# First-layer activations of token tiles five to nine and the scaling of rows on ScalarE instead of VectorE, with a planner that reckons with later landings

## The chip, the cores and the metric

The kernel runs on one core of a Trainium2 chip. A core has five instruction streams: PE (TensorE, matrix products; its weight loads are shown as PEld), DVE (VectorE), ACT (ScalarE), POOL (GpSimd) and SP (SyncE, which here issues nearly all transfers). The metric is the device time of one execution in microseconds (us); lower is better. Runs of this kernel differ by about 0.2%, which is about what a measurement can tell from no change.

## What is computed

Two layers of a diffusion backbone over 1024 latent tokens and 256 context tokens, width 1024, in float32. Cut to what matters here:

```python
for i in range(2):
    mod_x = silu(c) @ w_mod[i] + b_mod[i]          # shift, scale, gate for the latent tokens
    mod_c = silu(c_ctx) @ w_mod[i] + b_mod[i]      # and for the context tokens
    hx = rms_norm(x, norm_g[i]) * (1 + sc_x) + sh_x
    hc = rms_norm(ctx, norm_g[i]) * (1 + sc_c) + sh_c
    if i == 0:   # grouped-query attention, 16 heads on 4 key/value heads, per-head norm of q and k, 2-D rotary
        yx, yc = gqa_axial_mixer(hx, hc, a_w_in, a_q_norm_g, a_k_norm_g, a_w_out, cos, sin, True)
    else:        # neighbourhood attention (8 x 16 window plus all context tokens) with a position bias
        yx, yc = neighbourhood_mixer(hx, hc, b_w_in, b_rpb, b_w_out, False)
    # each mixer: (attention * silu(z)) @ w_out
    x = x + g_x * yx
    ctx = ctx + g_c * yc     # first layer only
return rms_norm(x, final_norm_g)
```

## The kernel before

Tokens lie in ten tiles of 128: tiles 0 to 7 are the latent tokens, 8 and 9 the context. A float32 operand of a product is split into two float16 parts, hi and lo, and a product is three matmuls (hi*hi, hi*lo, lo*hi).

**The first stage** (to about 100 us) loads `w_m0` (the modulation weights), the tokens and the key/value weights, and makes the first layer's input and its keys and values. `ln_pre(t)` loads a token tile, takes the sum of squares on ACT (L867), the inverse root on POOL (L660), and scales the rows in place by that factor on DVE (L869). `mod_cols` gives, for each block `kt` of 128 channels, the scale and shift columns `acol` and `scol`. `h_kt(t0, n, kt)` then makes one block of the input for `n` token tiles: PE transposes into a PSUM bank `pl` (L876), ACT writes hi as scale times value plus shift (L881), DVE writes the same in float32 into `tf` (L882), and DVE subtracts hi to get lo (L883):

```python
S.activation(hi[:, kt, c], pv, AF.Identity, scale=a, bias=b)      # L881
V.tensor_scalar(tf, pv, a, b, op0=ALU.mult, op1=ALU.add)          # L882
V.tensor_tensor(lo[:, kt, c], tf, hi[:, kt, c], op=ALU.subtract)  # L883
```

The calls are `h_kt(t, 1, 0)` for t = 0 to 3, `h_kt(0, 4, kt)` for kt = 1 to 7, `h_kt(4, 1, kt)`, `h_kt(5, 3, kt)` (384 columns) and `h_kt(8, 2, kt)` (256 columns) for all eight kt. The bank `pl` is one of two with the tag "pj". `kv_mm` multiplies the input with the key/value weights (PE L887, accumulators `pkv`), `kv_post` normalises and rotates k (mostly DVE), and `load_w` splits weights (ACT L730, DVE L731; `wkv`, then `wa` for the queries).

**The first layer** (about 100 to 700 us) projects queries and gates (PE L1034, `pa`), forms scores (`pm` for row maxima, `st`), and attends. `q_att` does one head of each pair with queries on the partitions: scores (`qs`, L1186 and L1187), DVE copies them with a running maximum into `qpf` (L1190), ACT takes the exponentials into the float16 tile `qpp` and back into `qpf` (L1202, L1203), POOL subtracts for the lo part (L1130), SP transposes by DMA within the tile `qpp` (L1205), and PE multiplies with the values (`qpv`, L1211 and L1213). `qpp` has four buffers, `qpf` four.

**The turn of the layers** (about 700 to 810 us) does the output projection (`poa`, L1358), the second normalisation (`ln_rows`, `split_rows`: DVE L677, L678, L690), and the first products of the second layer in a Winograd-like scheme (`winograd`: banks `pwq0a`, `pwq0b`, `pwq0c`; ACT copies `e1q` from the first at L1457; DVE makes `w1q` and `w2q` from `e1q` and the second at L1461 and L1469, after which PE goes on in that bank, L1517).

**The second layer** (about 810 to 1300 us) projects (`pwq`, `pwv`) and attends (`b_att`): scores `bsn` and `bsc`, exponentials into `bph` on ACT, the lo part on POOL (L1130), a DMA transpose `bpht<-bph` on SP (L1641), and the product with the values (`bpv`, L1646 to L1649). `bph` has four buffers, `bpht` six. The last stage is the output projection `pob` (L1739) with the final norm.

**What sets the order.** `Planner` walks over all instructions, keeps a modelled clock for each engine, and lays each engine's instructions in the order in which its model starts them; `apply` then pins this order on every queue. `cost` gives each instruction's modelled occupancy and latency; `schedule` adds semaphore delays, buffers, and for transfers a landing time: a DMA is taken to be usable 1500 ns after its share of the DMA engines is through. `deadlines` works out by when each instruction is needed so that PE does not wait, with a margin, and `refine` plans five more times with these due times as the rank, keeping the shortest plan. So an edit to the planner moves instructions on all five queues of the whole program.

Of the kernel before, what the change touches and what calls it, by code (L numbers as in the profile page):

```python
# [15 lines left out]
AF = mybir.ActivationFunctionType  # L16
ALU = mybir.AluOpType
# [25 lines left out]
class Planner:  # L43
# [2 lines left out]

    ENG = {"PE": "PE", "DVE": "DVE", "Activation": "ACT", "Pool": "POOL", "SP": "SP"}
    AHEAD = 2000.0
    SEM = {"PE": 60.0, "DVE": 35.0, "ACT": 35.0, "POOL": 80.0, "SP": 30.0}

    def __init__(self, tc, first=0):
# [64 lines left out]
    def cost(self, x, rd, wr):  # L116
# [6 lines left out]
        if e == "PE":  # L123
            f32 = ins[0].dtype == mybir.dt.float32
            cols = self.elems(outs[0])
            passes = (2 if x.is_transpose else 4) if f32 else 1
            if f32 and any("idf" in a.bass_ap.tensor.name for a in ins):
                passes = 2
            return max(cols * passes / 2.4 + 2.5, 29.0), 170.0
        if k == "InstDmaTransposeAnt":  # L130
            m = 1
            for s, c in list(ins[0].ap):
# [155 lines left out]
        self.gone = set(gone)  # L288

    def schedule(self, key=None, margin=0.0, scale=None):  # L290
        scale = scale or {}
        N = len(self.node)
        rank = key or (lambda i: i)
        key = lambda i: -1 if i in self.glued else rank(i)
# [20 lines left out]
        t = dict.fromkeys(engs, 0.0)  # L315
# [40 lines left out]
        while count < N:  # L356
# [43 lines left out]
            if e == "PE":  # L400
                ts, tp = tuple(x.tile_size or (128, 128)), tuple(x.tile_position or (0, 0))
                if pe_last and pe_last[0] != ts:
                    s += 97
                fin = s + occ + lat
                if ts[1] < 128 and pe_last and pe_last[0] == ts and pe_last[1] != tp:
                    t[e] = max(s + 7, t[e])
                    pe_hold = max(pe_last[2], s + occ)
                    t[e] = s + 7
                    pe_last = (ts, tp, pe_hold)
                else:  # L410
                    if pe_last and pe_last[0] == ts and ts[1] < 128:
                        pass
                    t[e] = s + (occ if ts[1] == 128 else occ / 4)
                    pe_last = (ts, tp, s + occ)
            elif type(x).__name__ in ("InstDMACopy", "InstDmaTransposeAnt"):
                t[e] = s + occ
                dma = max(dma, s + occ) + lat
                fin = dma + 1500
            else:
                t[e] = s + occ  # L420
                fin = s + occ + lat
# [34 lines left out]
    def deadlines(self, margin):  # L456
# [4 lines left out]
        for a in self.order["PE"]:  # L461
            idle += max(0.0, start[a] - prev)
            prev = max(prev, start[a] + (cst[a][0] if tuple(self.node[a].tile_size or (128, 128))[1] == 128
                                         else cst[a][0] / 4))
            due[a] = start[a] - idle
        heirs = collections.defaultdict(list)
        for i, names in self.came.items():
# [56 lines left out]
def trunk_kernel(ctx, tc, x, cx, cc, norm_g, ng_row, b_cols, sel_c, w_m0, w_mb, b_mod, a_wkv, a_wq, a_qg, a_kg, a_w_out,  # L524
# [337 lines left out]
    def ln_pre(t):  # L862
        xt = xstage[t] if t < NX else lp.tile([P, D], F32, name=f"xt{t}", tag="xt", bufs=2)
        DM.dma_start(xt, x[t * P:(t + 1) * P, :] if t < NX else cx[(t - NX) * P:(t - NX + 1) * P, :])
        jk = lp.tile([P, D], BF16, name=f"xj{t}", tag="xj", bufs=1)
        ss = lp.tile([P, 1], F32, name=f"xss{t}", tag="lss", bufs=2)
        S.activation(jk, xt, AF.Square, accum_out=ss)  # L867
        rs = rstd_from(lp, ss, 1, 1.0 / D, EPS, "ln")
        V.tensor_scalar_mul(xt, xt, rs[:, 0:1])  # L869
        xts[t] = xt  # L870

    def h_kt(t0, n, kt):
# [6 lines left out]
        pv = ps.rearrange("p a b -> p (a b)")  # L879
        a, b = acol[0][:, kt, s:s + 1], scol[0][:, kt, s:s + 1]  # L880
        S.activation(hi[:, kt, c], pv, AF.Identity, scale=a, bias=b)  # L881
        V.tensor_scalar(tf, pv, a, b, op0=ALU.mult, op1=ALU.add)  # L882
        V.tensor_tensor(lo[:, kt, c], tf, hi[:, kt, c], op=ALU.subtract)  # L883

    def kv_mm(ps, t, kt):
# [959 lines left out]
```

## Time and profile before

| what | us |
|---|---|
| median of 3 runs | 1345.55 (1344.1 to 1347.17) |
| the profiled execution | 1345.52 |
| its span, first to last instruction | 1343.7 |
| mean granted TensorE clock | 0.992 of full speed |

The profiled execution's own time lies 1.8 us above its span; the span is what the views divide up. "PE busy" counts the modelled duration of pipelined matmuls, so a short wait between two of them may not show as idle. In the busy tenths PE is at 8 or 9 in every one of 40 slices but the last (6); DVE stands at 79% of the span, ACT at 72%, POOL at 66%.

### The profile page before, as it was taken

What the parts mean: (1) busy time and instruction counts of PE and PEld (TensorE: products, weight loads), DVE (VectorE), ACT (ScalarE), POOL (GpSimd) and SP (SyncE); (2) the same over time, 40 slices, a digit from 0 to 9 for tenths busy, and PEclk for the clock granted to TensorE, in tenths of its full rate; (3) what the DMA queues carried; (4) which work ended last, traced back from release to release, by engine and by line L of the source; (5) the groups of instructions that cost most, each with busy time, mean ns of one, the idle gap of its engine ahead of it and who ended that gap; (6) DMA issues with size and microseconds to landing.
All of it is one profiled execution on the core that took longest, in us unless ns stands there. A gap on an engine that the chain in (4) does not pass through costs nothing.

```text
span 1343.7 us, 38645 instructions
## 1 busy us (share of the span) xinstructions
PE 1309.6 (97%) x15100; PEld 928.6 (69%) x15100; DVE 1067.1 (79%) x2456; ACT 969.0 (72%) x2076; POOL 891.2 (66%) x1214
## 2 busy tenths in 40 slices
PE   8999999999999999999999989999999999999996
PEld 4457777777777777776654457869687786968552
DVE  5898787888889787769528997878888888887665
ACT  4554889988888777798743456878878888887453
POOL 2323878777777767687876467677676868767543
PEclk9899999999999999999999999999999999999998
DMA  9633576786675222244317962678777877669952
GB/s 371 188 116 96 111 152 117 145 187 135 140 145 122 74 67 72 59 119 108 113 51 187 243 139 82 125 145 152 150 139 142 158 143 162 145 151 226 286 130 110
DMA packets 390496, 191.64 MB, mean 143 GB/s; under 512 B 349792, under 2 KB 355104, under 8 KB 390312
## 3 DMA queue, kind: packets, MB, share of 16 engines
q1 hardware_dynamic: 389736, 189.13, 62.1%
q8 instruction: 118, 1.93, 0.6%
q14 instruction: 66, 0.54, 0.1%
q10 hardware_dynamic: 576, 0.03, 0.0%
HBM read 91.03 MB, written 15.75 MB: 79 GB/s over the span
## 4 chain that ended last, share of the span: by engine, by line
PE 73%; DVE 10%; ACT 6%; DMA 5%; issue 3%; POOL 2%; DVEq 0%; POOLq 0%; SPq 0%; ACTq 0%
PE pa L1034 13%; PE poa L1358 6%; PE pob L1739 6%; PE st L1260 3%; PE st L1261 3%; PE pm L1068 3%; PE pkv L887 2%; PE pv L1137 2%; PE pv L1138 2%; PE pv L1136 2%; DMA bpht<-bph 2%; DMA qpp<-qpp 2%; PE pvc L1577 1%; PE qpv L1211 1%; PE pbc L1527 1%
## 5 line engine op out<-in xcount | busy, mean ns | idle before, releaser
L1130 POOL TENSOR_TENSOR pl<-pf,ph 128x256 f16<-128x256 f32 x400 | 274.9, 711 | 85.7 <-ACT pf L1247 56.2
L1130 POOL TENSOR_TENSOR bph<-bpf,bph 128x256 f16<-128x256 f32 (+1 forms) x224 | 184.0, 848 | 102.0 <-ACT bpf L1637 81.8
L1034 PE MATMUL pa<-wa,x 128*128 128x256 f16 x1536 | 219.8, 272 | 0.7 <-DVE q L822 0.7
L1245 ACT ACTIVATE ph<-st 128x512 f16<-128x512 f32 x240 | 143.8, 602 | 58.0 <-PE st L1261 56.2
L1565 PEld LDWEIGHTS <-hx 128*128 128x128 f16 x2688 | 157.3, 98 | 10.2 <-issue 1.3
L1034 PEld LDWEIGHTS <-x 128*128 128x128 f16 x1536 | 140.4, 97 | 33.3 <-issue 1.4
L1247 ACT ACTIVATE pf<-st 128x512 f32<-128x512 f32 x240 | 143.6, 604 | 2.0 <-DVE pl L1127 0.9
L1069 DVE TENSOR_REDUCE mxp<-pm 128x1 f32<-128x512 f32 x192 | 127.3, 683 | 12.8 <-PE pm L1068 11.7
L1137 PE MATMUL pv<-v,ph 128*128 128x64 f16 x960 | 122.4, 195 | 0.0
L1136 PE MATMUL pv<-v,ph 128*128 128x65 f16 x960 | 121.9, 193 | 0.2 <-ACT ph L1245 0.2
L1138 PE MATMUL pv<-v,pl 128*128 128x65 f16 x960 | 121.3, 192 | 0.0
L1130 POOL TENSOR_TENSOR qpp<-qpf,qpp 128x256 f16<-128x256 f32 (+1 forms) x158 | 93.4, 616 | 31.6 <-ACT qpf L1203 29.3
L1517 PEld LDWEIGHTS <-wb 128*128 128x128 f16 x672 | 63.9, 98 | 71.9 <-issue 6.6
L1635 ACT ACTIVATE bph<-bpf,bnx 128x384 f16<-128x384 f32 (+1 forms) x128 | 69.3, 581 | 52.4 <-DVE bnx L1627 33.8
L1136 PEld LDWEIGHTS <-ph 128*128 128x128 f16 x960 | 90.9, 97 | 22.1 <-ACT ph L1245 0.7
L1137 PEld LDWEIGHTS <-ph 128*128 128x128 f16 x960 | 90.4, 97 | 15.8 <-issue 0.4
L1138 PEld LDWEIGHTS <-pl 128*128 128x128 f16 x960 | 91.2, 99 | 9.3 <-POOL pl L1130 1.2
L1260 PE MATMUL st<-q,k 128*128 128x512 f16 x240 | 90.8, 379 | 0.7 <-ACT pf L1247 0.4
L1261 PE MATMUL st<-q,k 65*128 65x512 f16 x240 | 91.5, 381 | 0.0
L1358 PE MATMUL poa<-woa,oa 128*128 128x512 f16 x384 | 89.8, 379 | 0.0
L1739 PE MATMUL pob<-wob,obf 128*128 128x512 f16 x336 | 80.5, 379 | 1.9 <-DVE acc L1742 1.4
L1434 POOL TENSOR_TENSOR wtb<-wsb 128x256 f32<-128x256 f32 x64 | 56.5, 884 | 32.5 <-DMA wsb<-in_b_wp 17.0
(485 smaller groups left out, 4050.2 us busy)
## 6 DMA issues: line engine op xcount, KB each, us to landing
wg<-in_w_mb SPq DMA_DIRECT2D x32, 512.0 KB, 4.5
wsb<-in_b_wp SPq DMA_DIRECT2D x64, 256.0 KB, 2.8
wm<-in_w_m SPq DMA_DIRECT2D x16, 512.0 KB, 9.0
wsa<-in_a_wq SPq DMA_DIRECT2D x32, 256.0 KB, 3.5
xstage<-in_x SPq DMA_DIRECT2D x8, 512.0 KB, 5.6
wsoa<-in_a_w_out SPq DMA_DIRECT2D x16, 256.0 KB, 2.7
x<-in_x SPq DMA_DIRECT2D x8, 512.0 KB, 8.5
x_d<-x SPq DMA_DIRECT2D x8, 512.0 KB, 5.1
```

Of the source, the lines that this page charges most:

```text
L1034: T.matmul(ps[:, :, i, :], hA(a, kt, t), wt[w][:, kt, :], start=n == 0, stop=n == 3 * KT - 1)
L1130: G.tensor_tensor(lo[:, c], p32[:, c], hi[:, c], op=ALU.subtract)
L1136: T.matmul(pv[:, t, :], hi[:, c], v[:, 0:65], start=first and t == 0, stop=False)
L1137: T.matmul(pv[:, t, 0:HD], hi[:, c], v[:, 65:129], start=False, stop=False)
L1138: T.matmul(pv[:, t, :], lo[:, c], v[:, 0:65], start=False, stop=last and t == n - 1)
L1245: S.activation(ph, st, AF.Exp)
L1247: S.activation(p32, st, AF.Exp)
L1260: T.matmul(so, k1[:, g, kc], q1[:, :, i, :], start=True, stop=False)
L1261: T.matmul(so, k2[0:65, g, kc], q2[0:65, :, i, :], start=False, stop=True)
L1358: T.matmul(ps, lhs(a, kt), w[b][:, kt, :], start=n == 0, stop=n == 3 * KT - 1)
L1565: T.matmul(ps[:, t * P:(t + 1) * P], hx[a][:, t, blk, kt], wt[j][:, s_, w, kt], start=first and t == 0 and m == 0, stop=last and t == 3 an ...
L1739: T.matmul(ps, ob[kt][:, t, a], wout["b"][hf][b][:, kt, :], start=n == 0, stop=n == 3 * len(kts) - 1)
```

## The change

Three things, of which the third moves everything:

1. In `ln_pre` the scaling of the rows stays on DVE for tiles 0 to 3 and goes to ACT for tiles 4 to 9 (six instructions of 1024 columns, in place).
2. In `h_kt` the float32 copy `tf` stays on DVE for t0 below 5 and goes to ACT for the calls with t0 = 5 and 8 (eight instructions of 384 columns and eight of 256).
3. The planner: a transfer is taken to be usable 2000 ns, a DMA transpose 3000 ns, after its share of the DMA engines (before: 1500 ns for both); DVE, ACT and POOL are taken to be 2% slower; small matmuls cost a little more; a matmul on a 32-column part of the array holds PE for 0.3 of its cost (before: 7 ns, or a quarter); and the margin of the due times falls from 300 to 200 ns.

```diff
+    LAND = (2000.0, 3000.0)
+    SLOW = {"DVE": 1.02, "ACT": 1.02, "POOL": 1.02}
...
-            return max(cols * passes / 2.4 + 2.5, 29.0), 170.0
+            return max(cols * passes / 2.4 + 2.5, 140.0 if f32 and cols < 8 else 30.4), 170.0
...
-        scale = scale or {}
+        scale = scale or self.SLOW
...
-                    t[e] = s + 7
+                    t[e] = s + 0.3 * occ
...
-                fin = dma + 1500
+                fin = dma + self.LAND[type(x).__name__ == "InstDmaTransposeAnt"]
...
-                                         else cst[a][0] / 4))
+                                         else cst[a][0] * 0.3))
...
-        V.tensor_scalar_mul(xt, xt, rs[:, 0:1])
+        if t < 4:
+            V.tensor_scalar_mul(xt, xt, rs[:, 0:1])
+        else:
+            S.activation(xt, xt, AF.Copy, scale=rs[:, 0:1])
...
-        V.tensor_scalar(tf, pv, a, b, op0=ALU.mult, op1=ALU.add)
+        if t0 < 5:
+            V.tensor_scalar(tf, pv, a, b, op0=ALU.mult, op1=ALU.add)
+        else:
+            S.activation(tf, pv, AF.Identity, scale=a, bias=b)
...
-        plan.refine(5, 100.0, 300.0)
+        plan.refine(5, 100.0, 200.0)
```

The new lines shift the numbers after them: L881 becomes L886, L882 becomes L888 and L890, L1461 becomes L1469, L1646 becomes L1654. Three places show how the order moves. In the names the digits say which one it is: `pl51` is the bank of `h_kt(5, 3, 1)`, `x10` the hi part of the second half of the tokens, `pkv0` the accumulator of token tile 0; what follows the underscore only numbers the tile.

**ACT in the first stage, about 53 us into the program.** Before:

```order
L881 ACTIVATE x10_105<-pl51_671,scol_98,acol_97 128x384
L881 ACTIVATE x10_105<-pl44_691,scol_98,acol_97 128x128
L891 CAST v1_126<-pkv0_238 128x4x64
L891 CAST v1_126<-pkv1_239 128x4x64
L891 CAST v1_126<-pkv2_240 128x4x64
L891 CAST v1_126<-pkv3_241 128x4x64
L730 ACTIVATE wa00_923<-wsa02_933 128x512
L881 ACTIVATE x10_105<-pl52_700,scol_98,acol_97 128x384
```

Now:

```order
L886 ACTIVATE x10_105<-pl51_671,scol_98,acol_97 128x384
L732 ACTIVATE wa10_1247<-wsa10_1249 128x512
L899 CAST v1_126<-pkv0_238 128x4x64
L890 ACTIVATE tf51_675<-pl51_671,scol_98,acol_97 128x384
L886 ACTIVATE x10_105<-pl44_691,scol_98,acol_97 128x128
L899 CAST v1_126<-pkv1_239 128x4x64
L797 ACTIVATE sq0_143<-pkv0_238 128x4x64
L886 ACTIVATE x10_105<-pl52_700,scol_98,acol_97 128x384
```

The `tf` of each block now stands behind its hi on ACT, and a split of query weights (`wa10`) that came later stands between them.

**DVE at the turn of the layers, where PE waits for `w1q`.** Here `x18` is context tile 8, normalised in place in two halves. Before:

```order
L677 SCALAR_TENSOR_TENSOR x18_14222<-x18_14222,rs_ln_14451,lrow11_14445 128x512 x2
L678 TENSOR_TENSOR x18_14222<-x18_14222,lrow01_14443 128x512 x2
L658 TENSOR_SCALAR ms_ln_14470<-lssb9_14468 128x1
L690 TENSOR_TENSOR hrb81_14442<-x18_14222,hrb80_14441 128x512
L1461 TENSOR_TENSOR w1q0_14499<-e1q0_14484,pwq0b_14486 128x512
```

Now:

```order
L679 SCALAR_TENSOR_TENSOR x18_14222<-x18_14222,rs_ln_14451,lrow11_14445 128x512
L1447 SCALAR_TENSOR_TENSOR wb011_14639<-wtb010_14641,wb011_14639 128x4x128
L680 TENSOR_TENSOR x18_14222<-x18_14222,lrow01_14443 128x512
L679 SCALAR_TENSOR_TENSOR x18_14222<-x18_14222,rs_ln_14451,lrow11_14445 128x512
L1469 TENSOR_TENSOR w1q0_14499<-e1q0_14484,pwq0b_14486 128x512
L680 TENSOR_TENSOR x18_14222<-x18_14222,lrow01_14443 128x512
L692 TENSOR_TENSOR hrb81_14442<-x18_14222,hrb80_14441 128x512
```

`w1q` has moved ahead of the second half of the shift and of the first lo part.

**PE in the second layer, ahead of the values of one transposed tile** (`bpht112`: pair 1, head 1, token tile 2; `bsn107` and `bsc106` are scores for later tiles, `pwv2a` and `pwv2b` products for the next pair). Before, with twelve matmuls into `pwv2a` between the two groups shown:

```order
L1598 MATMUL bsn107_16995<-bk11_15143,bq11_15142 128x256
L1599 MATMUL bsn107_16995<-bk11_15143,bq21_13810 128x256
...
L1646 LDWEIGHTS bpht112_16710
L1646 MATMUL bpv110_16548<-bv11_15144,bpht112_16710 128x65
```

Now, with 24 matmuls (three into `pwv2a`, 21 into `pwv2b`) between them:

```order
L1606 MATMUL bsc106_17017<-bk11_15143,bq11_15142 128x256
L1607 MATMUL bsc106_17017<-bk11_15143,bq21_13810 128x256
...
L1654 LDWEIGHTS bpht112_16710
L1654 MATMUL bpv110_16548<-bv11_15144,bpht112_16710 128x65
```

The product with this tile now stands behind the scores `bsc106` and more of the next pair's products; it has moved later on PE. Of the 128 tiles `bpht` 104 have more PE work between their own scores and their product than before, of the 96 tiles `qpp` 89.

## The prediction

> **What bounds the kernel now.** I read the page's summary first, then the windows with the granted clock, then the table of waits, and last the single places.
>
> ```profile
> span 1343.7 us, 38645 instructions
> PE 1309.6 (97%) x15100; PEld 928.6 (69%) x15100; DVE 1067.1 (79%) x2456; ACT 969.0 (72%) x2076; POOL 891.2 (66%) x1214
> 1332.29 0.81 PE L1739 MATMUL pob<-wob,ob 128*128 128x512 f16 x3
> ```
>
> PE bounds the kernel: it is idle for 1343.7 - 1309.6 = 34.1 us in all. Of this the tail takes 1343.7 - 1333.1 = 10.6 us, since the last matmuls start at 1332.29 and run 0.81 us. The change removes no matmul. So what it can win is a part of the other 23.5 us, and time that PE loses to a lowered clock. The windows (columns: width, busy time of PE, PEld, DVE, ACT, POOL with counts, granted clock, DMA share, GB/s) show where both lie:
>
> ```profile
> core 0: us, PE busy (x) PEld busy (x) DVE busy (x) ACT busy (x) POOL busy (x), PEclk, DMA share, GB/s
> 15.00:25.00 10.00, 10.00 (x77) 5.17 (x79) 6.02 (x17) 2.60 (x5) 0.00 (x0) 0.85 1.03 407
> 45.00:65.00 20.00, 17.27 (x90) 8.68 (x88) 18.54 (x44) 13.82 (x30) 8.57 (x9) 0.85 0.42 64
> 50.00:66.00 16.00, 13.28 (x55) 6.46 (x54) 14.78 (x37) 10.53 (x24) 9.12 (x8) 0.79 0.52 80
> 60.00:65.00 5.00, 4.53 (x13) 1.93 (x12) 4.64 (x13) 2.24 (x5) 1.26 (x1) 0.50 0.30 42
> 774.00:798.00 24.00, 20.39 (x92) 9.00 (x91) 21.86 (x33) 12.38 (x22) 15.70 (x17) 0.93 0.56 118
> ```
>
> From 50 to 66 us PE is idle for 16.00 - 13.28 = 2.72 us and runs at 0.79 of its clock, which costs another 0.21 x 16 = 3.4 us: 6.1 us in one stage, with DVE busy for 14.78 of 16. From 774 to 798, the turn of the layers, it is 3.61 us idle and 0.07 x 24 = 1.7 us by the clock: 5.3. From 15 to 25 the transfers run at a share of 1.03, so the start is bound by loading. The waits say who is late (last columns: us in total, times, longest):
>
> ```profile
> PE bpv L1646 <- DMA bpht<-bph: 3.5, 5, 1.0
> PE pkv L887 <- ACT x L881: 2.5, 3, 1.5
> PE pwq0b L1517 <- DVE w1q L1461: 2.2, 1, 2.2
> PE pl L876 <- DVE tf L882: 1.0, 2, 0.7
> PE qpv L1211 <- DMA qpp<-qpp: 0.9, 2, 0.7
> PEld L1646 <- DMA bpht<-bph: 4.8, 7, 1.2
> PEld L1211 <- DMA qpp<-qpp: 4.0, 8, 1.2
> ```
>
> The matmuls' rows are a lower bound (pipelining hides the first part of a wait), the weight loads' rows an upper one. Transposed tiles that land too late are the largest wait in both.
>
> **Part one, the moved instructions.** Their prices, and the nearest rows for those that ACT does not yet do:
>
> ```profile
> L882 DVE TENSOR_SCALAR tf<-pl,acol,scol 128x384 f32<-128x384 f32 x8 | 5.3, 668 | 1.0 <-ACT x L881 1.0
> L882 DVE TENSOR_SCALAR tf<-pl,acol,scol 128x256 f32<-128x256 f32 x8 | 4.2, 539 | 0.1
> L881 ACT ACTIVATE x<-pl,scol,acol 128x384 f16<-128x384 f32 x8 | 5.4, 670 | 4.7 <-PE pl L876 4.7
> L881 ACT ACTIVATE xc_hi<-pl,scol,acol 128x256 f16<-128x256 f32 x8 | 4.4, 560 | 1.4 <-PE pl L876 1.3
> L869 DVE TENSOR_SCALAR xstage<-xstage,rs_ln 128x1024 f32<-128x1024 f32 x8 | 6.0, 755 | 1.0 <-POOL rs_ln L660 1.0
> L869 DVE TENSOR_SCALAR xt<-xt,rs_ln 128x1024 f32<-128x1024 f32 x2 | 2.5, 1258 | 0.2 <-POOL rs_ln L660 0.2
> L867 ACT ACTIVATE xj<-xt 128x1024 bf16<-128x1024 f32 x2 | 2.1, 1048 | 0.0
> L1750 ACT ACTIVATE jk<-acc x16: 613/629/631, 1294.0 to 1334.0; 128x512 f32<-128x512 f32 x16
> L1758 ACT ACTIVATE acc<-acc,rs_fin x7: 706/722/722, 1297.4 to 1334.6; 128x512 f32<-128x512 f32 x7
> ```
>
> DVE loses 5.3 + 4.2 + 4 x 0.755 + 2.5 = 15.0 us. ACT gains, for the sixteen `tf`, 5.4 + 4.4 = 9.8 us (the same form with a float16 output). A row scaling of 1024 columns on ACT is not in the trace: at least 1.05 us (L867, same width, no scale column), at most 2 x 0.722 = 1.44. I take 0.722 + (1.048 - 0.629) = 1.14, since doubling the width costs L1750 to L867 just that; six are 6.8 us. ACT gains 16.6 us. [...]
>
> What it is worth is read from 50 to 66 us, where PE waits behind DVE (`tf`, L882) and ACT (`x`, L881). With DVE relieved, the bank `pl` is freed by ACT alone. ACT is busy 13.82 of 20 us from 45 to 65; about seven of the 384-column `tf` and one scaling fall there, 7 x 0.67 + 1.14 = 5.8 us, which makes 19.6 of 20. So DVE stops being the bound and ACT all but becomes it. The gain lies between nothing and the whole 6.1; I take half, **-3.0**. What hides the added ACT work is its 6.2 us of idle time there; without that cover it would cost its full 5.8 us. Queued behind each `tf` on ACT are the k and v casts and the splits of query weights; the latter are needed only once the projection `pa` starts.
>
> ```profile
> wm<-in_w_m SPq DMA_DIRECT2D x16, 512.0 KB, 9.0
> ```
>
> On SP the first key/value weight `wskv0` now stands behind two more of these loads, 1 MB. At 407 GB/s that is 2.6 us later for the first `pkv`, but the second block of modulation, ahead of it on PE now, was due to run anyway, and what follows waits for loading. Between 0 and 2.6: **+0.5**.
>
> **Part two, the turn of the layers.**
>
> ```profile
> 774.11 0.68 DVE L1439 SCALAR_TENSOR_TENSOR wb<-wtb,wb 128x512 f16<-128x512 f32 x1
> 776.80 0.63 ACT L1438 ACTIVATE wb<-wtb 128x512 f16<-128x512 f32 x1 [1.87 <-POOL wtb L1436]
> 777.34 0.57 ACT L1457 COPY e1q<-pwq0a 128x512 f32<-128x512 f32 x1
> 777.96 1.24 PE L1517 MATMUL pwq0a<-hx,wb 128*128 128x512 f16 x5 [1.00 <-ACT e1q L1457]
> 784.90 1.79 DVE L678 TENSOR_TENSOR x<-x,lrow 128x512 f32<-128x512 f32 x2
> 786.68 0.87 DVE L690 TENSOR_TENSOR hrb<-x,hrb 128x512 f16<-128x512 f32 x1
> 788.21 0.81 PE L1517 MATMUL pwq0b<-hx,wb 128*128 128x512 f16 x3 [2.15 <-DVE w1q L1461]
> 798.43 0.27 PE L1527 MATMUL pbc<-hc,wb 128*128 128x256 f16 x1
> 790.00:795.00 5.00, 4.54 (x18) 1.92 (x17) 4.52 (x9) 2.35 (x5) 0.00 (x0) 0.72 0.75 163
> ```
>
> `w1q` now overtakes half of L678 (0.9 us) and one L690 (0.87): 1.8 us earlier against a wait of 2.15. A split of weights such as that at 774.11 (0.68) now stands among what is ahead of it, in the place of small things; I count 1.6. On ACT `e1q` no longer stands behind a split (the one at 776.80, which itself waited for POOL): `e1q` could start 0.5 us earlier, against PE's wait of 1.00. The clock of 0.72 right behind the wait is then likely spared (1.7). The sum is **-3.8**, between nothing and 5.3. The overtaken lo part of the context, which ended at 787.55, is late next, by the 0.68 of `w1q`; what is made from it goes into `pbc`, which PE starts at 798.43, so 10 us cover it.
>
> **Part three, the later landings.**
>
> ```profile
> L1641 SPq DMA_TRANSPOSE bpht<-bph x112: 1231/1348/2457, 833.7 to 1236.6; - x112
> DMA to landing us min/median/max: 3.1/3.6/5.2
> L1202 ACT ACTIVATE qpp<-qpf,qnx x96: 491/716/797, 132.4 to 417.4; 128x512 f16<-128x512 f32 x64, 128x256 f16<-128x256 f32 x32
> L1211 PE MATMUL qpv<-v,qpp x320: 217/221/232, 141.2 to 426.1; 128*128 128x128 f16 x160
> ```
>
> A transpose lands 3.1 to 5.2 us after its issue; the planner now allows 1.5 us more, and no single wait for one exceeds 1.2 us. So most vanish where PE has other work to put first, as in the third order shown. The waits are worth 3.5 to 4.8 us for `bpht` and 0.9 to 4.0 for `qpp`; since a few tiles did not move back, I take 3.4 and 0.8: **-4.2**, between nothing and 8.8.
>
> **Part four, what a new order gives back.** 23.5 us of PE idle less 2.7, 3.6 and 4.4 in the places above leaves some 12.8 us of small waits and of the start. All five queues are laid anew, with a thinner margin (200 ns for 300), and matmuls on 32 columns are priced higher. I add a quarter, **+3.0**, between -3 and +8.
>
> The sum: 1345.5 - 3.0 + 0.5 - 3.8 - 4.2 + 3.0 = **1338.0 us**, against the profiled execution's own 1345.52 (the median is 1345.55, so no shift).
>
> **Rivals.**
>
> *The buffers run out (slower).* A tile `qpp` is held from its exponential to its product: 141.2 - 132.4 = 8.8 us, at the last tile 426.1 - 417.4 = 8.7. Four buffers at (417.4 - 132.4)/95 = 3.0 us a tile allow 12.0. With 1.5 us more, 10.3 are used. Past 12.0 each tile's period grows by a quarter of the excess; at 12.5 that is 96 x 0.125 = 12 us, and ACT, then `qpf` on DVE, then the score banks stop PE: 1338.0 + 12 = **1350**. For it: the gap is not wide. Against it: the planner counts the four buffers itself. 0.12.
>
> *ACT becomes the bound of the first stage.* Its densest five microseconds there are:
>
> ```profile
> 50.00:55.00 5.00, 4.45 (x26) 2.48 (x25) 4.14 (x10) 4.38 (x10) 4.70 (x4) 1.00 0.61 95
> ```
>
> At 4.38 of 5 (88%), 19.6 us of work take 22.3: 2.3 us longer than before in place of 3.0 shorter, **1343.3**. For it: `tf` now waits behind `hi` on one queue. Against: the weight splits could wait. 0.11.
>
> *The clock still falls.* The half clock came at 60 us though no wait there exceeded 1.5 us, so single long gaps are not its cause, and small ones remain; then 1.7 us at the turn and about 1.8 of the first stage are not won: **1341.5**. 0.09. [...]
>
> *The landings move along.* If a transpose is late because SP and the DMA engines are behind, and not because PE asks early, part three is nothing: **1342.2**. The spread of 3.1 to 5.2 us speaks for it, the short waits against it. 0.09.
>
> *The whole gain.* Parts one and two in full and nothing given back: 1338.0 - 3.1 - 1.5 - 3.0 = **1330.4**. 0.12.
>
> **How the numbers follow.** The forecast has 0.47, with its own range 1333 to 1342. A measurement here tells about 0.2% (2.7 us) from no change. Faster: 0.47 + 0.09 + 0.09 + 0.12 = 0.77; same: 0.10 and slower 0.13, the case of ACT giving 0.10 to the one and, with the buffers' 0.12, 0.01 to the other. The range runs from 1331, just above the whole gain, to 1346, past ACT as the bound; it leaves out the buffers and the best cases.
>
> **What would show it.** Right: from 50 to 66 us PE busy above 14.5 with a clock above 0.9, ACT above 85%; the wait of `pwq0b` for `w1q` under 1 us; the waits of L1654 for `bpht` under 1.5 us in total. Wrong: PE waiting for score banks or for `qpf` between 130 and 430 us (buffers); `pl` or `pkv` waiting for ACT for more than 4 us (ACT); the same waits for `bpht` at longer landings.

## The result, and the profile after

The changed kernel takes as long as the kernel before: a median of 1346.23 us (1343.26 to 1349.4, 12 runs) against 1345.88 (1343.2 to 1348.71, 12 runs), a ratio of 1.0001 with a 95% interval of 0.999 to 1.0012. Forecast were 1338.0. The profiled execution of the changed kernel is its fastest (1343.26 us, span 1341.5), so a difference of 2 us between this profile and that of before tells nothing. What tells is the places. (Of all the runs used below one, with the planner's edits alone at a margin of 220 ns, took 2329.16 us; it is left out of its kernel's ratio.) First the summary of the changed kernel's page and the rows of its table of waits that matter here (us in total, times, longest):

```profile
span 1341.5 us, 38632 instructions
PE 1307.4 (97%) x15100; PEld 929.3 (69%) x15100; DVE 1061.2 (79%) x2434; ACT 981.1 (73%) x2098; POOL 893.9 (67%) x1214
PE pwv0c L1573 <- DVE wb L1447: 2.8, 2, 2.5
PE pl L881 <- ACT tf L890: 2.6, 1, 2.6
PE pwv0c L1573 <- ACT wb L1446: 2.3, 1, 2.3
PE st L1268 <- ACT pf L1255: 1.8, 4, 0.7
PE bsn L1606 <- DVE bmx L1625: 1.5, 3, 0.7
...
PE qpv L1219 <- DMA qpp<-qpp: 0.5, 2, 0.3
...
PE pwq0b L1525 <- DVE w2q L1477: 0.3, 1, 0.3
```

PE's wait for `bpht` (3.5 us before) and that of `pwq0b` for `w1q` (2.2) are gone from the list, as forecast. At its head stand three rows that were not there. Two are of `pwv0c`, the bank of the first products of the second layer's values, for split weights `wb`: 5.1 us at the turn of the layers. One is of the transposes into `pl` for `tf`, now written by ACT: 2.6 us in the first stage. The two stages in the windows (width, busy time of PE, PEld, DVE, ACT and POOL with counts, granted clock, DMA share, GB/s):

```profile
50.00:66.00 16.00, 12.84 (x62) 6.74 (x61) 14.08 (x35) 13.81 (x31) 3.22 (x4) 0.89 0.82 211
774.00:798.00 24.00, 17.91 (x88) 8.06 (x87) 23.21 (x34) 12.18 (x22) 15.05 (x19) 1.00 0.54 121
```

From 50 to 66 us PE is idle for 3.16 us against 2.72, at a clock of 0.89 against 0.79. Counted as the prediction counts it, idle time and lowered clock together, the loss there is 3.16 + 0.11 x 16 = 4.9 us against 6.1. At the turn PE is idle for 6.09 us against 3.61, at full clock, so 6.1 against 5.3, and DVE is busy for 23.21 of 24 us. Both places were to be won.

A wait is only the part of a loss that shows as idle. To compare whole plans I take from each trace the time from the start of one matmul to the start of the next beyond the pace of its form (0.216 us for 512 columns and 0.109 for 256, the median steps in the traces before and after, and so on), which counts waits and lowered clock alike. All kernels here have the same 1277.1 us of matmuls by that pace, so the stages can be cut at equal work. The limits in the table are therefore us of matmul work and not places in the profile: the column of the turn spans about 750 to 857 us of the run. PE's stalls in us:

| kernel (margin of due times, ns) | first stage, 0 to 100 us of work | first layer, 100 to 550 | its end, to 700 | turn, to 800 | second layer, to 1150 | end | sum |
|---|---|---|---|---|---|---|---|
| before (300) | 17.5 | 15.7 | 4.6 | 6.8 | 5.7 | 3.9 | 54.2 |
| changed (200) | 14.8 | 16.3 | 5.7 | 7.5 | 3.4 | 3.9 | 51.7 |
| changed, second profile | 16.2 | 15.8 | 5.3 | 7.6 | 3.2 | 5.1 | 53.2 |

### The profile page after: what moved, and what is told of

The parts are those of the page before. It is cut to its first block, busy times and chain, and to the rows that moved or that the text cites. A ratio compares the mean times of both kernels' runs of the same rounds, so it can differ in the third digit from the quotient of the medians.

```text
span 1341.5 us, 38632 instructions
## 1 busy us (share of the span) xinstructions
PE 1307.4 (97%) x15100; PEld 929.3 (69%) x15100; DVE 1061.2 (79%) x2434; ACT 981.1 (73%) x2098; POOL 893.9 (67%) x1214
## 5 line engine op out<-in xcount | busy, mean ns | idle before, releaser
L1042 PE MATMUL pa<-wa,x 128*128 128x256 f16 x1536 | 223.6, 272 | 0.0
L1144 PE MATMUL pv<-v,ph 128*128 128x65 f16 x960 | 124.7, 193 | 0.1
L1138 POOL TENSOR_TENSOR qpp<-qpf,qpp 128x256 f16<-128x256 f32 (+1 forms) x158 | 96.3, 632 | 37.3 <-ACT qpf L1211 24.1
L1145 PEld LDWEIGHTS <-ph 128*128 128x128 f16 x960 | 90.6, 97 | 16.9
```

The lines of the kernel that those rows point to most:

```text
L1042: T.matmul(ps[:, :, i, :], hA(a, kt, t), wt[w][:, kt, :], start=n == 0, stop=n == 3 * KT - 1)
L1138: G.tensor_tensor(lo[:, c], p32[:, c], hi[:, c], op=ALU.subtract)
L1144: T.matmul(pv[:, t, :], hi[:, c], v[:, 0:65], start=first and t == 0, stop=False)
L1145: T.matmul(pv[:, t, 0:HD], hi[:, c], v[:, 65:129], start=False, stop=False)
```

## The experiments

All ratios are to the kernel before, run beside each kernel on the same chip. Line numbers differ by a few between kernels. The theories: **A**, the moves pay and the planner's edits lose it; **B**, the moves put ScalarE's queue in PE's way; **C**, every new plan wins and loses somewhere, whatever is edited; **D**, the gain is lost at the two places above; **E**, the moves cost some 4 us under the new planner; **F**, the later landings are what wins; **G**, the turn is full of work, so that no order wins there.

### Each half of the change alone

`moves_only` is the kernel before with the six scalings and sixteen `tf` on ScalarE; `plan_only` is the changed kernel with them on VectorE:

```diff
-        if t0 < 5:
-            V.tensor_scalar(tf, pv, a, b, op0=ALU.mult, op1=ALU.add)
-        else:
-            S.activation(tf, pv, AF.Identity, scale=a, bias=b)
+        V.tensor_scalar(tf, pv, a, b, op0=ALU.mult, op1=ALU.add)
```

> The kernel before with the moved instructions alone (the row scaling of tiles 4 to 9 and the sixteen tf on ScalarE); planner as before. Theory A (the moves pay, what they win is lost by the planner's edits): 2 to 3 us faster than before, PE busy above 14.0 us from 50 to 66 us, the waits for bpht still 3 us or more in total on the matmuls. Theory B (the moves put ScalarE's in-order queue in PE's way): no gain or up to 3 us slower, and PE waits for pl or pkv behind ACT for 2 us or more between 45 and 70 us. Theory C (every new plan loses about as much as it wins, wherever it is changed): within 1.5 us of before, with a different list of places where PE waits.

> The changed planner alone, tf and the row scaling back on VectorE. Theory A (the landings pay as forecast, the loss sits at the moved instructions): waits for bpht under 1 us in total, and 3 to 4 us faster than before. Theory C (what the later landings win is lost at other places that the new plan serves worse): waits for bpht under 1 us all the same, but the time within 1.5 us of before, and PE's waits for other things 3 us or more above those of before.

`moves_only`: 0.9999 (0.999 to 1.0007). `plan_only`: 0.9973 (0.9964 to 0.9983), 1340.63 us, so 0.27% faster. The waits of `moves_only`, then the window from 50 to 66 us of `moves_only` and of `plan_only`:

```profile
PE bpv L1652 <- DMA bpht<-bph: 3.3, 6, 1.3
PE qpv L1217 <- DMA qpp<-qpp: 3.1, 7, 0.7
```

```profile
50.00:66.00 16.00, 13.07 (x69) 6.35 (x68) 14.60 (x39) 15.60 (x36) 6.08 (x6) 1.00 0.47 86
```

```profile
50.00:66.00 16.00, 14.25 (x77) 6.97 (x76) 15.46 (x39) 9.63 (x22) 3.59 (x5) 1.00 0.68 148
```

With the moves alone PE's stalls of the first stage fall from 17.5 to 13.8 us, at full clock. But the planner's edits alone bring them to 14.1 without any move, and then ACT is busy for only 9.63 of 16 us. In these profiles the two halves of the change win much the same 3 to 4 us, and with both the stage stands at 14.8, so their gains do not add. The waits for `bpht` stay in `moves_only` and fall to 0.2 us in `plan_only`.

For `moves_only` theory A foretold 2 to 3 us less and PE busy above 14.0 us in the window; neither came. The sign of theory B, waits behind ACT, parts nothing: those of `pkv` are 3.1 us over the whole run, where the kernel before has 2.5, and the stalls of the stage fell all the same. Theory C has the time right. `plan_only` is 4.5 us faster than the kernel before beside it (1345.13 us), as theory A said and C did not.

### Repairing the two places by hand

`rep12` keeps the changed kernel's plan and moves thirteen instructions within it. Shown are the VectorE and ScalarE ones; on PE, three matmuls into `pwv0c` go behind `pwq0c` ones and five behind `pwq0b` ones:

```diff
         plan.refine(5, 100.0, 200.0)
+        shift(plan, 'ACT', (('wa10_', 'wsa10_'), 0), (('tf52_', 'pl52_'), 0))
+        shift(plan, 'DVE', (('wa11_', 'wsa10_'), 0), (('x11_', 'tf52_'), 0))
+        shift(plan, 'DVE', (('w1q0_',), 0), (('wb011_', 'wtb010_'), 0))
+        shift(plan, 'DVE', (('w2q0_', 'e1q0_'), 0), (('hrb81_', 'x18_'), 0))
+        shift(plan, 'DVE', (('c22q0_', 'w2q0_'), 0), (('x19_', 'lrow11_'), 0))
```

> The changed kernel with its plan kept and only thirteen instructions moved by hand within it: the split of wa10 on ScalarE and VectorE stands behind the tf of pl52, and at the turn of the layers w1q, w2q and c22q stand ahead of the context's normalisation on VectorE and eight matmuls pwv0c behind the pwq0b ones on PE. Theory D (the gain was lost at these two places, behind weights that land late): the waits of 2.6 us (pl for tf) and of 5.1 us (pwv0c for wb) fall to less than 1.5 us together, and the kernel is 4 to 6 us faster than the changed one, 1340 to 1342. Theory C (a stall that is taken away at one place comes back at the next): these waits go, but PE's waits in the 40 us behind each place grow by as much, and the time is within 1.5 us of the changed kernel's.

Measured: 0.9997 (0.9988 to 1.0006). What it repairs in the first stage is best seen in the timeline of the changed kernel's ACT and PE (start, duration, and in brackets the idle time and who ended it):

```profile
53.50 0.68 ACT L886 ACTIVATE x<-pl,scol,acol 128x384 f16<-128x384 f32 x1
56.16 0.63 ACT L732 ACTIVATE wa<-wsa 128x512 f16<-128x512 f32 x1 [1.98 <-DMA wsa<-in_a_wq]
56.69 0.35 ACT L899 CAST v<-pkv 128x256 f16<-128x256 f32 x1
56.94 0.68 ACT L890 ACTIVATE tf<-pl,scol,acol 128x384 f32<-128x384 f32 x1
57.67 0.69 PE L881 MATMUL pl<-idf,xstage 128*128 128x128 f32 x2 [2.58 <-ACT tf L890]
```

ACT is not short of time here: it stands for 1.98 us before a split of query weights whose load has not landed, and the `tf` that frees `pl` stands behind that split. With the split moved behind this `tf` and the next one, the stage becomes what was forecast (`rep12`, window 50 to 66 us):

```profile
50.00:66.00 16.00, 14.57 (x78) 7.14 (x77) 15.96 (x41) 15.97 (x35) 2.99 (x4) 1.00 0.75 174
```

PE 14.57 us, clock 1.00, ACT busy throughout. The stalls of the first stage are 12.9 us (14.8 and 16.2 in the changed kernel's two profiles), and of the wait of 2.6 us 0.2 is left. So the cause of this wait is shown. At the turn the repair failed:

```profile
784.59 0.22 PE L1573 MATMUL pwv0c<-wb,hx 128*128 128x128 f16 x1 [2.04 <-ACT wb L1446]
788.17 2.75 PE L1525 MATMUL pwq0b<-hx,wb 128*128 128x512 f16 x12 [0.78 <-DVE w2q L1477]
792.98 0.33 PE L1573 MATMUL pwv0c<-wb,hx 128*128 128x128 f16 x3 [2.05 <-DVE wb L1447]
```

The same products wait for the same splits, now until 784.59 and 792.98 us (782.65 and 792.42 in the changed kernel), with a longer wait for `w2q` between; the waits for `wb` are 4.3 us in place of 5.1, and the turn's stalls rise from 7.5 to 9.6 us. Theory D's explanation holds for the first place and falls for the second, and its 4 to 6 us did not come: at 1345.32 us the time is within theory C's 1.5 us of the changed kernel's.

### Is the turn full? Less work, same order

Two kernels keep every instruction of the changed kernel in its place, but cut eight instructions of the context's normalisation on VectorE (`short_dve`), or four of its residual sum on GpSimd (`short_pool`), to 4 columns. The planner is told the cost of 512 columns, so the order does not change. The second pair of lines is `short_dve`'s, the third `short_pool`'s:

```diff
-        n = max([self.elems(a) for a in outs + ins] or [1])
+        n = max([self.elems(a) for a in outs + ins] or [1]); n = 512 if n == 4 and outs[0].bass_ap.tensor.name[:4] in ("x18_", "x19_") else n
...
-            V.scalar_tensor_tensor(xt[:, c], xt[:, c], rs[:, 0:1], lrows[1][:, c], op0=ALU.mult, op1=ALU.mult)
+            c = slice(hf * 512, hf * 512 + (4 if v else 512)); V.scalar_tensor_tensor(xt[:, c], xt[:, c], rs[:, 0:1], lrows[1][:, c], op0=ALU.mult, op1=ALU.mult)
...
-            (V if t == NX - 1 else G).tensor_tensor(x1[:, hc], x1[:, hc], tm, op=ALU.add)
+            m = slice(0, 512 if t < NX else 4); (V if t == NX - 1 else G).tensor_tensor(x1[:, hc][:, m], x1[:, hc][:, m], tm[:, m], op=ALU.add)
```

> The changed kernel with its plan unchanged, but the scaling and the shift of the context rows ahead of the second layer (eight VectorE instructions of 512 columns, some 6.7 us at the turn of the layers) cut to 4 columns each, so most of that normalisation is left out. Theory G (VectorE's work fills the turn, so an order cannot win there, and w1q's wait had to come back elsewhere): the wait of pwv0c for the split on VectorE at 789 us (2.8 us in the first profile, 1.3 in the second) and that for w2q (0.3) fall below 0.5 together, and PE's stalls from 774 to 800 us fall from 7.5 to 5 or less. Rival (the weights' transfers are late): they stay as they are.

> The changed kernel with its plan unchanged, but the residual sum of the two context tiles on GpSimd (four instructions of 512 columns, some 4.5 us at the turn) cut to 4 columns each, so most of that sum is left out. Theory G' (at the turn GpSimd is full too; ScalarE waits for its sum in L675 with the split of wb behind it): the wait of pwv0c for the split on ScalarE at 780 us (2.3 us in both profiles) falls below 0.5, and the one for VectorE shrinks too since wtb is ready earlier. Rival (order or late transfers alone): the 2.3 us stay.

Waits from 770 to 802 us and the window 774 to 800 us of `short_dve`:

```profile
PE pwv0c L1573 <- ACT wb L1446: 2.1, 1, 2.1
PE pwq0a L1525 <- ACT e1q L1465: 0.7, 1, 0.7
...
PE pwq0b L1525 <- DVE w2q L1477: 0.5, 1, 0.5
...
774.00:800.00 26.00, 22.38 (x128) 10.97 (x127) 20.36 (x37) 14.81 (x26) 15.77 (x21) 0.93 0.58 128
```

The same of `short_pool`:

```profile
PE pwv0c L1573 <- DVE wb L1447: 2.8, 2, 2.5
PE pwq0a L1525 <- ACT e1q L1465: 0.7, 1, 0.7
PE pwv0c L1573 <- ACT wb L1446: 0.3, 1, 0.3
...
774.00:800.00 26.00, 21.84 (x108) 9.84 (x106) 24.46 (x39) 14.84 (x26) 13.95 (x21) 0.93 0.65 141
```

Each takes away the wait of `pwv0c` that was foretold for it and leaves the other. Less work on VectorE ends the wait for its split (2.8 to nothing; `w2q` rose from 0.3 to 0.5). Less on GpSimd ends most of the wait for ScalarE's split (2.3 to 0.3), because ScalarE's sum of squares, which stood waiting for GpSimd ahead of that split, comes earlier. In the changed kernel:

```profile
780.93 1.06 ACT L675 ACTIVATE hrb<-x 128x1024 f16<-128x1024 f32 x1 [1.39 <-POOL x L1371]
781.99 0.61 ACT L1446 ACTIVATE wb<-wtb 128x512 f16<-128x512 f32 x1
```

In `short_pool` the product that waits for this split starts at 781.38 us after a wait of 0.34 us, in the changed kernel at 782.65 after 2.29. So both waits are made by work in the queues of VectorE and GpSimd at the turn, and late transfers are not their cause. Two expectations failed. In `short_pool` VectorE's wait did not shrink. And in `short_dve` the stalls did not fall to 5 us: over the whole turn they are 7.1, and 7.0 in `short_pool`, against 7.5 and 7.6 in the changed kernel's two profiles. From 774 to 800 us, idle time and lowered clock together are 3.62 + 0.07 x 26 = 5.4 us in `short_dve` and 4.16 + 1.8 = 6.0 in `short_pool`; the changed kernel has 6.1 at full clock and 4.64 + 1.8 = 6.5 in a second profile at the same 0.93 (both rows stand in the last section). So the work makes these waits, but taking it away won at most about 1 us of the stage; what holds the rest was not tried. Each kernel ran once, in 1342.43 and 1344.41 us.

### The same plan again

> The changed kernel once more, for a second profile of the same plan, since its first profile (span 1341.5 us) was the fastest of its twelve runs. If the places of the waits belong to the plan: the waits of 2.6 us at pl and of 5 us at pwv0c are there again within 0.5 us each, and another 2 to 4 us of waits or of lowered clock appear, since its usual run is longer. If they belong to the run: they are gone or elsewhere.

One run of the changed kernel, 1344.75 us. Its waits:

```profile
PE pl L881 <- ACT tf L890: 2.6, 1, 2.6
PE pwv0c L1573 <- ACT wb L1446: 2.3, 1, 2.3
PE st L1268 <- ACT pf L1255: 1.7, 4, 0.6
PE bsn L1606 <- DVE bmx L1625: 1.5, 3, 0.7
PE idle L843 <- DVE twos L586: 1.5, 1, 1.5
PE pwv0c L1573 <- DVE wb L1447: 1.3, 2, 1.1
```

Most waits repeat to 0.1 us: they belong to the plan. The waits of `pwv0c` do not: 3.6 us against 5.1, though half a microsecond was allowed. What differs besides is the start (14.8 and 16.2 us of stalls in the first stage), the end, and the split between idle time and clock at the turn. The stalls are 1.5 us more in all, below the 2 to 4 expected. Where the further 1.5 us up to the median of 1346.23 lie, neither profile shows.

### Other plans of the same program

The margin of the due times, moved by 1 to 100 ns, changes no instruction but lays the queues anew. It is the only edit by which ten more kernels differ from one already named, for instance:

```diff
-        plan.refine(5, 100.0, 300.0)
+        plan.refine(5, 100.0, 301.0)
```

`land_only` is the kernel before with the later landings alone:

```diff
+    LAND = (2000.0, 3000.0)
...
-                fin = dma + 1500
+                fin = dma + self.LAND[type(x).__name__ == "InstDmaTransposeAnt"]
```

`margin_201` and `margin_300` are draws of the changed kernel, `plan_only_*` of the changed planner without the moves, `before_*` of the old planner.

> The changed kernel with the margin of the due times at 201 ns in place of 200: an edit that means nothing, but lays the queues anew (some 4800 rows of PE's order differ). Theory C (the plan is a draw): the list of the places where PE waits changes, with single waits of 1 to 3 us that come and go, and the time is off by 1 to 4 us to either side. Theory D (the loss belongs to the change's own parts): the waits at 54 and at 780 to 793 us stay, and the time is within 1 us of the changed kernel's.

> The changed kernel with the margin of the due times at 300 ns as before: a third draw of moves and planner together. Theory E (the moves cost some 4 us under the new planner): 0.999 to 1.001 of before, as the first two draws (1.0001 and 0.9998). Theory C (draws scatter by 0.2 to 0.4%): anywhere from 0.997 to 1.002. If it is the thinner margin that takes the gain back: 0.9965 to 0.998.

> The changed planner without the moves, at a margin of 201 ns in place of 200: a second draw of the kernel that was 0.9973 of before. Theory E (the moved instructions cost some 4 us under the new planner, whatever the draw): 0.9965 to 0.998 of before again, 1340 to 1342 us. Theory C (the 0.9973 was one good draw of plans that scatter by 0.2 to 0.4%): anywhere from 0.997 to 1.001, and clearly nearer to 1 than the first draw.

> The changed planner without the moves at a margin of 220 ns: a third draw (some 6400 rows of PE's order differ from the first), after 0.9973 and 0.9987. If the planner's edits win on the mean: 0.997 to 0.999. If the first two were luck: 0.999 to 1.002. Waits for bpht under 1 us in total either way.

> The changed planner without the moves at a margin of 190 ns: a fourth draw, after 0.9973, 0.9987 and 1.0011. If the planner's edits win on the mean: 0.997 to 1.000. If there is no win on the mean: 1.000 to 1.002. PE's waits for bpht under 1 us in total either way.

> The kernel before with the later landings alone (2000 ns for transfers, 3000 for transposes); the moves, the engines' 2 per cent, the prices of small matmuls and the margin as before. Theory F (the landings are what the planner's edits win): waits for bpht under 1 us in total, and 0.9965 to 0.998 of before. Rival (the win is in the other edits of the planner): bpht's waits go, but the time stays within 0.1 per cent of before.

> The later landings alone, at a margin of 301 ns in place of 300: a second draw of the kernel that was 1.0019 of before. If the landings help on the mean of draws: 0.997 to 1.0005, below the first draw. If they cost (a later landing asked everywhere makes the turn of the layers worse: 10.9 us of PE's stalls there in the first draw against 6.8 before): 1.001 to 1.003 again, with 9 us or more at the turn.

> The kernel before with the margin of the due times at 301 ns in place of 300: a second draw of the old planner (some 2300 rows of PE's order differ). Theory C (plans scatter by 0.1 to 0.3%, the verdict of no change is partly a matter of the draw): 0.997 to 1.003, not 1 within its interval in one case of two; waits for bpht 3 us or more again. Rival (small edits of the plan do not matter): 0.999 to 1.001.

> The kernel before at a margin of 290 ns in place of 300: a third draw of the old planner. Theory C' (the kernel before is a good draw of the old planner, and the change is held against that draw, not against the planner): slower than before by 0.1 to 0.4 per cent, 1347 to 1351 us, as at 301. Rival (301 was one bad plan): 0.999 to 1.001.

> The kernel before at a margin of 320 ns: a fourth draw of the old planner. Theory C': 1.001 to 1.004 of before. Rival: 0.999 to 1.001. In both, waits for bpht of 3 us or more in total.

> The moves alone under the old planner at a margin of 310 ns: a second draw, after 0.9999. If the moves pay on the mean of old plans (the three fresh ones lie at 1.0017 to 1.0037): 1.0015 or less. If they pay nothing: 1.002 to 1.004. Waits for bpht of 3 us or more in both.

> The fastest kernel so far once more, unchanged (planner's edits without the moves, margin 200 ns; 0.9973 of before, interval 0.9964 to 0.9983). It was the best of four plans, so part of its lead may be chance of measurement. If the lead belongs to the plan: 0.9965 to 0.998 again. If it was a lucky set of runs: 0.9985 to 1.000.

Ratios with intervals, and PE's stalls in us from one profile each (the sum has the two stages that are not shown; two profiles of one plan differ by up to 1.5 us in a column):

| planner | moves | margin | ratio (95%) | first stage | first layer | turn | second layer | sum |
|---|---|---|---|---|---|---|---|---|
| old | no | 300 | 1 | 17.5 | 15.7 | 6.8 | 5.7 | 54.2 |
| old | no | 290 | 1.0017 (1.0005 to 1.003) | 19.3 | 15.9 | 7.7 | 5.2 | 56.8 |
| old | no | 301 | 1.0028 (1.0017 to 1.0039) | 16.2 | 21.1 | 6.9 | 5.6 | 59.0 |
| old | no | 320 | 1.0037 (1.0022 to 1.0052) | 18.6 | 16.9 | 6.2 | 7.5 | 59.4 |
| old | yes | 300 | 0.9999 (0.999 to 1.0007) | 13.8 | 17.2 | 7.9 | 6.5 | 53.4 |
| old | yes | 310 | 1.0039 (1.0026 to 1.0053) | 13.8 | 18.9 | 9.7 | 7.2 | 59.1 |
| landings only | no | 300 | 1.0019 (1.0008 to 1.003) | 15.1 | 17.0 | 10.9 | 3.2 | 56.4 |
| landings only | no | 301 | 1.0008 (0.9996 to 1.002) | 15.3 | 20.6 | 9.9 | 2.4 | 54.6 |
| new | no | 190 | 0.9981 (0.9969 to 0.9994) | 14.2 | 19.7 | 7.2 | 1.3 | 52.0 |
| new | no | 200 | 0.9973 (0.9964 to 0.9983) | 14.1 | 17.6 | 7.3 | 1.8 | 49.2 |
| new | no | 200, again | 0.9959 (0.9947 to 0.9972) | 14.2 | 16.1 | 7.4 | 1.8 | 48.4 |
| new | no | 201 | 0.9987 (0.9977 to 0.9997) | 14.2 | 16.4 | 8.7 | 2.7 | 53.2 |
| new | no | 220 | 1.0011 (0.9999 to 1.0023) | 14.8 | 17.1 | 8.6 | 4.1 | 56.8 |
| new | yes | 200 | 1.0001 (0.999 to 1.0012) | 14.8 | 16.3 | 7.5 | 3.4 | 51.7 |
| new | yes | 201 | 0.9998 (0.9986 to 1.001) | 12.9 | 17.7 | 8.8 | 3.7 | 53.9 |
| new | yes | 300 | 0.9993 (0.9981 to 1.0005) | 12.4 | 18.3 | 10.4 | 2.5 | 54.6 |

One nanosecond of margin makes the old kernel 0.28% slower. The head of the table of waits of that kernel (old planner, 301 ns):

```profile
PE qpv L1211 <- DMA qpp<-qpp: 6.0, 6, 1.7
PE bpv L1646 <- DMA bpht<-bph: 3.1, 5, 0.9
PE pwq0b L1517 <- DVE w1q L1461: 2.2, 1, 2.2
```

The wait for `w1q` is that of before and that for `bpht` nearly so; what is new is 6.0 us (0.9 before) for `qpp`, at places of the first layer that no edit touched.

What the columns say, from the top. The second layer's stalls are 5.2 to 7.5 us in all six kernels without the later landings and 1.3 to 4.1 in all ten rows with them: theory F holds for this stage. The turn leans the other way, with much overlap: 6.2 to 9.7 without, 7.2 to 10.9 with. There PE waits for `w1q` or, in `pwv0c`, for split weights in every one of the sixteen profiles of the table, 2.2 to 5.4 us in all from 770 to 802 us; the kernel before has the least, all of it for `w1q`. The wait for `w1q` is not gone for good either: in the changed kernel at 300 ns it is 3.9 us, with 0.7 for split weights. The first layer scatters from 15.7 to 21.1 without and from 16.1 to 20.6 with, and the kernel before has the lowest value of the table.

Of the old planner's four plans that of before is the fastest; the mean of the four is 1.0021. The mean of the new planner's four without the moves (0.9966 for the one run twice) is 0.9986. The four plans of each side scatter with standard deviations of 0.0016 and 0.0019, so the standard error of the difference, 0.0034 or 4.6 us, is 0.0012. With the moves the mean of three is 0.9997: they win nothing that shows, with either planner, and that they cost something under the new one (theory E) is not settled by three plans against four. Held against the mean of the old planner's four plans, and not against the best of them, the changed kernel too is ahead, by 1.0021 - 0.9997 = 0.0024 or 3.2 us, with a standard error of about 0.0008 from the scatter of the plans. The landings alone (1.0019 and 1.0008) do not make the kernel faster than before, nor clearly faster than the old planner's mean; so theory F fails for the time. This suggests that the planner's other edits have their part in the lead of `plan_only`, but none of them was tried apart.

How the other expectations came out. In `margin_201` the wait at 54 us nearly went (0.7 us left), the waits of `pwv0c` stayed, and the time hardly moved, so neither C nor D is wholly right. `margin_300` (0.9993) does not show that the thinner margin took the gain back. Of the new planner's draws without the moves the second (0.9987) lies outside what theory E foretold and the third (1.0011) outside a win on the mean, the fourth (0.9981) inside. The old planner's three fresh draws came out as theory C said, but at 320 ns the waits for `bpht` were 1.3 us and not 3. The moves at 310 ns (1.0039) did not pay. `land_only` lies outside both of its ranges; its second draw (1.0008) lies between its two, with the dear turn (9.9 us) of the one that has the landings cost time.

**A version that beats both**: the planner's edits without the moves, at 200 ns. It was the best of four, but kept its lead in a second set of runs: 0.9973 and 0.9959 of before, 1340.63 and 1340.36 us.

## Why the prediction was wrong

Forecast were 7.5 us less. By the stalls of the first table, the four parts (the whole first layer counted with the last) measured -2.7 + 0.7 - 2.3 + 1.7 = -2.6 us in the one profile and -1.3 + 0.8 - 2.5 + 2.0 = -1.0 in the other; by the medians nothing was won (+0.35 us), and neither profile shows where the rest went. The step that failed is part two, 4.5 us off and of the wrong sign.

**Part one, -3.0 and +0.5.** The prices were right: the sixteen `tf` take 9.8 us on ACT as worked out, a scaling 1.14 as taken:

```profile
L890 ACT ACTIVATE tf<-pl,scol,acol 128x384 f32<-128x384 f32 (+1 forms) x16 | 9.8, 620 | 0.0
L874 ACT ACTIVATE xstage<-xstage,rs_ln x4: 1137/1138/1141, 29.4 to 42.2; 128x1024 f32<-128x1024 f32 x4
```

The whole first stage won 2.7 us in the one profile and 1.3 in the other, near the 2.5 forecast. That is partly luck: the planner's edits without any move won 3.4 there, which the working did not foresee, and from 50 to 66 us, where PE was to be busy for more than 14.5, only about 1.2 were won in the one profile and 0.5 in the other. The working named what is queued behind each `tf` on ACT and dismissed the weight splits as "needed only once the projection `pa` starts". They matter not for who needs them but for where they stand: one stood ahead of a `tf` and waited for its load. `rep12` shows the forecast state of the stage once it is out of the way, though not a shorter run. The shift of `wskv0` was not told apart from the rest of the start.

**Part two, -3.8: the step that failed.** The working had the overtaking of `w1q` shorten the turn. The turn measured +0.7 and +0.8 in the two profiles. `w1q` did overtake and its wait did vanish, just as reasoned; but "10 us cover it" was said of the context alone. The weight splits for `pwv0c`, one of which the working had itself counted ahead of `w1q`, were what came late next: 5.1 and 3.6 us of waits in place of 2.2. The quoted row had a hint in it: DVE busy for 21.86 of 24 us. In this stage, with an engine at 91%, what one instruction won by overtaking, others in the queues of VectorE and ScalarE lost; with less work the awaited split came in time, with another order it did not (`short_dve`, `short_pool`, `rep12`). The clock was spared in the first profile (1.00), with no gain: see the last section.

**Part three, -4.2.** The mechanism was right, the size too large. For `bpht` 3.4 was forecast; PE's waits for it are at most 0.3 us in every plan with later landings, and the second layer's stalls fell by 2.3 and 2.5 us in the changed kernel, while waits for `bmx` (1.5) and others came up there. For `qpp` 0.8 was forecast and nothing came: its waits fell from 0.9 to 0.5, but the first layer's stalls went from 15.7 to 16.3 and 15.8.

**Part four, +3.0.** First layer, its end and the end of the kernel gave back 0.6 + 1.1 + 0.0 = 1.7 us in the one profile and 0.1 + 0.7 + 1.2 = 2.0 in the other.

**What no step had.** The kernel before is one draw of its planner, and of four the fastest. A forecast that adds up repaired places of that draw leaves out that a new plan also loses what the old one had by luck: 2.6 to 5.2 us of stalls by the sums in the table (54.2 against 56.8, 59.0 and 59.4). How much of the miss is this was not measured apart from the rest. Part four was meant to hold this, but was sized from the small waits of the good draw.

**The rivals.** The buffers did not run out: between 130 and 430 us no wait of PE for score banks or `qpf` exceeds 0.5 us. ACT as the bound was the nearest to the truth in its place but not in its mechanism: PE waited for ACT for 3.2 us there (2.6 at `pl`, 0.6 at `pkv`), under the 4 set as the mark, with ACT blocked and not full; when it was full (`rep12`, 15.97 of 16) PE did not suffer (14.57 of 16). The clock from 50 to 66 us rose to 0.89 and not above 0.9, and at the turn it fell in one of the two profiles: the rival on the clock was right in this, but its 1341.5 us falls short of the miss, and at the turn the clock cost nothing; that small gaps make it fall, as this rival took, no run shows. The landings did not move along with PE's demand: PE's waits for `bpht` went from 3.5 us to 0.3 at most.

## What to carry to other kernels

Where a planner lays out the whole program, measure a change on several plans of each side (here a margin moved by a few ns) before believing or dropping it: here single plans of one planner differ by up to 0.4%, as much as all that the edits won. A wait in a stage where another engine is over 90% busy (here VectorE, 21.86 and 23.21 of 24 us) was not won here by moving the awaited instruction forward: the next one in the queue came late. Less work on that engine ended the wait (2.8 us to nothing), but even so most of the stage's loss stayed (5.4 us of 6.1 and 6.5). When work is moved onto a queue whose order is pinned, look for instructions ahead of it that wait for a transfer: here such a one, with ScalarE idle for 1.98 us before it, and not the queue's busy time, set when the work ran.

## What the runs showed of the hardware

A lowered clock cost nothing at the turn of the changed kernel, where PE waits for another engine anyway. The turn of the same plan, 774 to 800 us, in the first and in the second profile:

```profile
774.00:800.00 26.00, 19.91 (x111) 9.52 (x110) 24.98 (x37) 14.13 (x25) 16.88 (x21) 1.00 0.56 123
```

```profile
774.00:800.00 26.00, 21.36 (x101) 9.54 (x100) 24.71 (x37) 13.37 (x24) 16.02 (x21) 0.93 0.55 122
```

At full clock PE is idle for 26.00 - 19.91 = 6.09 us, at 0.93 for 4.64, and the stalls of the whole turn by the measure above are 7.5 and 7.6: the slower matmuls fill the wait for VectorE (the waits of `pwv0c` for its split are 2.8 us in the one, 1.3 in the other). This speaks against counting the clock's 1.7 us there as a gain of its own, as the prediction did.

The clock also fell at the end of a single wait of 2.58 us in the first stage of the changed kernel (windows):

```profile
57.00:57.60 0.60, 0.00 (x0) 0.00 (x0) 0.60 (x2) 0.60 (x3) 0.00 (x0) 1.00 0.80 114
57.70:60.00 2.30, 2.30 (x7) 1.09 (x7) 2.30 (x8) 2.20 (x6) 0.10 (x1) 0.50 0.87 246
```

and where that wait was taken out (`rep12`) it stayed at 1.00. PE's matmuls around the wait:

```profile
53.10 1.89 PE L895 MATMUL pkv<-wkv,x 128*128 128x512 f16 x8
54.83 0.27 PE L881 MATMUL pl<-idf,xstage 128*128 128x128 f32 x1
57.67 0.90 PE L881 MATMUL pl<-idf,xstage 128*128 128x128 f32 x3 [2.58 <-ACT tf L890]
58.37 1.06 PE L895 MATMUL pkv<-wkv,x 128*128 128x512 f16 x2
```

In the kernel before the clock is at half by 58.95 us, behind single waits of 0.74 and 0.67 us, and no wait of PE from 45 us to there is longer:

```profile
54.06 1.68 PE L887 MATMUL pkv<-wkv,x 128*128 128x512 f16 x7
56.47 0.66 PE L876 MATMUL pl<-idf,xstage 128*128 128x128 f32 x4 [0.74 <-DVE tf L882]
57.79 0.94 PE L887 MATMUL pkv<-wkv,x 128*128 128x512 f16 x3 [0.67 <-DVE x L883]
58.95:60.00 1.05, 0.96 (x5) 0.82 (x5) 1.05 (x5) 0.21 (x2) 0.00 (x0) 0.50 0.47 43
```

So in this stage the half clock stood behind a wait of 2.58 us in the one kernel and behind waits of 0.74 us at most in the other. What sets the moment, no run here shows.
